# A two-layer stream encoder on one core: the guard of a hand-made instruction order counts engine time anew, the split of squares takes other tiles as room, and the start takes six small steps

## The chip, the cores and the metric

The kernel runs on one core of one Trainium2 chip. The metric is the device time of one execution in microseconds (us), as the median of several runs; lower is better.

## What is computed

The reference is an encoder of two layers on a sequence of 256 tokens of width 2048, all in float32. Cut to what matters:

```python
for l in range(2):
    h = rmsnorm(x, norm_mix[l])
    x = x + hybrid_mixer(h, ...)            # h @ w_in; three recurrences; concat([hg, ret, ssm]) @ w_out
    h = rmsnorm(x, norm_xattn[l]); m = rmsnorm(mem, norm_mem[l])
    x = x + memory_cross_attention(h, m)    # q = h @ wq; k, v = m @ wkv; softmax; @ wo
    x = x + conv_glu_ffn(rmsnorm(x, norm_ffn[l]))   # @ w_up, conv of 3 taps, silu(gate) * up, @ w_down
return rmsnorm(x, norm_final)
```

The mixer has three recurrences side by side: hg (a gated one), ret (a decaying one with rotary positions) and ssm. The output of each goes through a norm over groups before w_out.

## The kernel before, in words

**Work and stages.** Everything is kept transposed: channels on the 128 partitions, the 256 tokens in the free dimension. The weights, 479 MB in all, are streamed once from HBM through SyncE's DMA queue in groups of about 0.5 MB into five buffers `raw`. A float32 product is made of rounded pieces: ScalarE (ACT) rounds a piece of weights to `wh`, VectorE (DVE) subtracts to get the rest `wl`, and TensorE (PE) does, for each 128x128 block, one matmul of `wh` with 512 columns (the high and the low part of the activations beside each other) and one of `wl` with 256 columns. One such pair is called a pair below, one block of 128 channels of the input a k-tile.

**The order of the work.** The program is written out by hand, engine by engine; no scheduler moves anything, and every engine runs its own list in order. The main loop (from L1429) goes over some 890 steps, mostly of eight blocks: it issues the rounding of the weights of the step three ahead (`split_w_hi`, L1302) and the subtraction of the step two ahead (`split_w_lo`, L1310), which also loads a later group, then the step's matmuls, and then lets everything else move on by one piece. Because `wh` has five buffers and `wl` four, `wh` for step j+3 can't be written before PE has finished step j-2. "Everything else" are Python generators: the evacuation of a finished product, a norm, a recurrence, the attention. `advance` (L341) calls each of them once per step, and each issues instructions up to its next `yield`.

**The guard.** `advance(False)` after a step skips a generator when the books say that ACT or DVE is more than `BACKLOG` = 10 us behind (L344); only evacuations of products are never skipped. The books are kept by `Metered` (L248), which adds for each instruction (columns + fixed) / rate, and by `step_done` (L351), which takes off the time of the step's matmuls, so many us for each block, and adds what is over to `late`. Where a matmul needs an input that no generator has issued yet, `need` (L357) calls `advance()` with the guard off until it is there, ahead of that matmul in all the lists; `pj` (L379) does the same when all five PSUM tiles for products are held.

**What the steps of the argument touch.** `gen_gstd` (L637) makes the norm over groups: it splits squares into a high and a low part, sums them over the partitions with two matmuls, and goes on into `newton` (L402: Ln and Exp on ACT, then three operations on DVE); `gen_out` (L614) then multiplies and splits the result into the inputs `mo` of w_out. `z_evac` (L819) holds the PSUM tiles of the products z4 to z7 until all of hg's outputs are issued (the flag `hgdone`). `gen_mem` (L1062) makes the normalized memory `mh` for k and v, two k-tiles from each fetched piece of `memT`; a piece goes into one of two buffers `ya`, and the fetch of the next but one is issued when both k-tiles are done. `gen_first` (L1396) makes the squares of x for the first norm, whose result R every product of the first layer's w_in is multiplied with. The tiles `pr` and `w` have two buffers each; `gen_out` uses `pr`, `newton` and the rotary part of `gen_ret` (L1001) use `w`. At the start the first `SINGLE` steps carry one k-tile instead of two; x is loaded in pieces by the same queue as the weights.

Of the kernel before, what the change touches and what calls it, by code (L numbers as in the profile page):

```python
# [5 lines left out]
F32R = mybir.dt.float32r  # L6
# [5 lines left out]
P = 128  # L12
T = 256
# [44 lines left out]
K16 = [list(range(8)), list(range(8, 16))]  # L58


SINGLE = 4


def layer_plan(l):
# [183 lines left out]
class Metered:  # L248


    def __init__(self, engine, rate, fixed, fast=()):
        self.engine, self.rate, self.fixed, self.fast, self.us = engine, rate, fixed, fast, 0.0

    def __getattr__(self, name):
        f = getattr(self.engine, name)
        if name == "preload_act_table_set":
            def g(*a):
                self.us += 1.28
                return f(*a)
            return g  # L260

        def g(out, *a, **k):
            n = 1
            for d in out.shape[1:]:
                n *= d
            self.us += (n / (2 if name in self.fast else 1) + self.fixed) / self.rate
            return f(out, *a, **k)  # L267
        return g


def build(tc, ws, xT, memT, par, con, masks, rot, dec, outT):
    nc = tc.nc
    act, dve, pe, gp = Metered(nc.scalar, 1200.0, 190), Metered(nc.vector, 960.0, 64, ("tensor_scalar",)), nc.tensor, nc.gpsimd

    pc = tc.alloc_tile_pool(name="const", bufs=1)
    pw = tc.alloc_tile_pool(name="weights", bufs=1)
# [46 lines left out]
    def tmp(tag, shape, dt=F32, bufs=2):  # L323
        return pt.tile(shape, dt, name=nm(tag), tag=tag, bufs=bufs)
# [9 lines left out]
    def start(g, first=False):  # L334

        if first:
            gens.insert(sum(f for _, f in gens), (g, True))
        else:
            gens.append((g, False))
# [28 lines left out]
    def take(n):  # L368
        while free["ms"] < n:
            yield  # L370
        free["ms"] -= n
# [26 lines left out]
    def tt(out, a, b, op):  # L398
        dve.tensor_tensor(out, a, b, op)


    def newton(v, out):  # L402

        fn(out, v, AF.Ln)
        fn(out, out, AF.Exp, scale=-0.5)
        yield
        t = tmp("w", [P, 2, T])
        t = t[:, 0, :] if len(v.shape) == 2 else t
        dve.scalar_tensor_tensor(t, out, -0.5, out, ALU.mult, ALU.mult)
        tt(t, t, v, ALU.mult)  # L410
        dve.scalar_tensor_tensor(out, t, 1.5, out, ALU.add, ALU.mult)
# [66 lines left out]
    lock = {}  # L478
# [67 lines left out]
    def layer(l):  # L546
# [89 lines left out]

        def gen_gstd(sq, n, v, out):  # L637

            while lock.get("pr", 0):
                yield  # L640
            lock["pr"] = 2
            hl = [tmp("pr", [P, 2, T], F32R, bufs=2) for _ in range(2)]
            split_ones(sq, *hl)
            yield
            yield from take(1)
            ps = bank()
            sum_ones(ps.rearrange("p (i t) -> p i t", i=2), *hl)
            lock["pr"] = 0
            yield
            dve.tensor_scalar(v, ps.rearrange("p (i t) -> p i t", i=2), 1.0 / n, EPS, ALU.mult, ALU.add)  # L650
            give()
            yield
            yield from newton(v, out)
# [347 lines left out]
        def gen_ret(p):  # L1001
# [10 lines left out]
            for name in ("rq", "rk"):  # L1012
                yield from wait((A, name, b0), (A, name, b1))
                if "R" not in ret:
                    ret["R"] = 1
                    tt(ret["cs"], ret["cs"], R.unsqueeze(1).to_broadcast([P, 2, T]), ALU.mult)
                U = pg[name][:, b0:b0 + 2, :]

                W = tmp("w", [P, 2, T])
                for o in (0, 64):  # L1020
                    act.copy(W[o:o + 64], U[64 - o:128 - o])
                tt(U, U, ret["cs"][:, 0:1, :].to_broadcast([P, 2, T]), ALU.mult)
                tt(W, W, ret["cs"][:, 1:2, :].to_broadcast([P, 2, T]), ALU.mult)
                tt(U, U, W, ALU.add)
                yield
# [4 lines left out]
            for i in range(2):  # L1030
                a = b0 + i
# [278 lines left out]
    def split_w_lo(j):  # L1310
        if j < len(steps):
            st = steps[j]
            n = st["n"]
            st["wl"] = pw.tile([P, WMAX], F32R, name=nm("wl"), tag="wl", bufs=4)
            tt(st["wl"][:, :n], st["raw"], st["wh"][:, :n].bitcast(F32), ALU.subtract)
            if j + 1 == len(steps) or steps[j + 1]["g"] != st["g"]:
                load(st["g"] + 5)
            if j < 4:
                nc.sync.dma_start(X[2 + j // 2][:, j % 2 * 2:j % 2 * 2 + 2, :], xT[:, 8 + 2 * j:10 + 2 * j, :])

    begins = {}
    done = []
# [43 lines left out]
    with tc.manual_schedule():  # L1366
# [5 lines left out]
        def loadx(q, a, b):  # L1372
            q.dma_start(X[a // 4][:, a % 4:(b - 1) % 4 + 1, :], xT[:, a:b, :])
# [3 lines left out]
        act.preload_act_table_set("silu_and_others")  # L1377
        table[0] = "silu_and_others"
        load(1)
        for a, b, g in ((2, 3, 2), (3, 4, 3), (4, 6, 4), (6, 8, None)):  # L1380
            loadx(nc.sync, a, b)
            if g:
                load(g)

        warm = bank()
        for _ in range(NWARM):
# [33 lines left out]
            flags.add("lb")  # L1420
            yield

        start(gen_first())
        for j in range(2):
            first_h(j)
            split_w_hi(j)
# [2 lines left out]
        for j, st in enumerate(steps):  # L1429
# [8 lines left out]
                start(ev(ps), True)  # L1438
            done.clear()
            matmuls(st)  # L1440
            if j == 5:
                fn(ONES, one, AF.Copy)
                nc.sync.dma_start(CON, con)
# [7 lines left out]
            if j == 15:  # L1451
                start(gen_lb())
            advance(False)
            step_done(st["n"] / P * 0.325)
        for ev, ps in done:
            start(ev(ps))
        start(gen_rstd((("Z",), "acc"), ACC, R, None, ("RZ",)))
# [36 lines left out]
```

## Time and profile before

| what | value |
|---|---|
| median of 3 runs | 2571.05 us (2569.22 to 2572.76) |
| the profiled execution | 2572.93 us, its span 2571.1 us |
| mean granted clock of TensorE | 0.996 of full speed |
| busy, share of the span | PE 99%, DVE 75%, ACT 57% |

The span runs from the first to the last instruction; the execution's time has some 2 us around it. A row of the timeline gives the start, the duration, the engine and what is written from what; in brackets stands the idle time of the engine before it and what ended it.

### The profile page before, as it was taken

What the parts mean: (1) busy time and instruction counts of PE and PEld (TensorE: products, weight loads), DVE (VectorE), ACT (ScalarE), POOL (GpSimd) and SP (SyncE); (2) the same over time, 40 slices, a digit from 0 to 9 for tenths busy, and PEclk for the clock granted to TensorE, in tenths of its full rate; (3) what the DMA queues carried; (4) which work ended last, traced back from release to release, by engine and by line L of the source; (5) the groups of instructions that cost most, each with busy time, mean ns of one, the idle gap of its engine ahead of it and who ended that gap; (6) DMA issues with size and microseconds to landing.
All of it is one profiled execution on the core that took longest, in us unless ns stands there. A gap on an engine that the chain in (4) does not pass through costs nothing.

```text
span 2571.1 us, 40478 instructions
## 1 busy us (share of the span) xinstructions
PE 2547.1 (99%) x15584; PEld 2259.8 (88%) x15584; DVE 1927.2 (75%) x3034; ACT 1469.6 (57%) x2154; POOL 5.0 (0%) x12
## 2 busy tenths in 40 slices
PE   9999999999999999999999999999999999999998
PEld 8888978898888888888898888889988888888887
DVE  6898788768776567776678888876787765677765
ACT  6766566566555345555466665655655543555543
POOL 0000000000000000000000000000000000000000
PEclk9999999999999999999999999999999999999999
DMA  7556555656665666666665576565666666666664
GB/s 265 163 172 203 192 171 189 192 170 189 190 191 181 194 194 189 191 189 188 191 184 161 154 235 186 184 217 169 181 189 190 192 182 193 193 189 192 190 184 130
DMA packets 141105, 482.03 MB, mean 187 GB/s; under 512 B 15280, under 2 KB 21360, under 8 KB 140912
## 3 DMA queue, kind: packets, MB, share of 16 engines
q1 hardware_dynamic: 140624, 479.17, 60.2%
q8 instruction: 123, 2.02, 0.3%
q14 instruction: 70, 0.57, 0.1%
q10 hardware_dynamic: 288, 0.27, 0.0%
HBM read 477.25 MB, written 2.13 MB: 186 GB/s over the span
## 4 chain that ended last, share of the span: by engine, by line
PE 97%; DVE 2%; DMA 0%; ACT 0%; issue 0%; DVEq 0%; SPq 0%; ACTq 0%
PE pj L1339 57%; PE pj L1340 29%; PE pj L1360 2%; PE pj L1361 2%; PE pj L1362 2%; PE pj L1342 1%; PE pj L1343 1%; PE pj L1344 1%; PE ms L694 1%; DVE wl L267 0%; PE ms L777 0%; PE ms L943 0%; DVE w L267 0%; PE ms L1131 0%; PE ms L1165 0%; DMA raw<-ws 0%
## 5 line engine op out<-in xcount | busy, mean ns | idle before, releaser
L1339 PE MATMUL pj<-H,wh 128*128 128x512 f32 x4480 | 1563.3, 393 | 1.6 <-DVE H L267 1.6
L267 DVE TENSOR_TENSOR wl<-raw,wh 128x1024 fp32r<-128x1024 f32 (+2 forms) x894 | 1076.1, 1206 | 420.8 <-PE pj L1340 221.6
L267 ACT ACTIVATE wh<-raw 128x1024 fp32r<-128x1024 f32 (+2 forms) x894 | 934.6, 1048 | 659.0 <-PE pj L1339 349.7
L1340 PE MATMUL pj<-H,wl 128*128 128x256 f32 x4480 | 1254.4, 280 | 3.4 <-DVE wl L267 3.4
L1339 PEld LDWEIGHTS pj<-H,wh 128*128 128x128 f32 x4480 | 842.0, 188 | 188.3 <-DVE H L267 1.4
L1340 PEld LDWEIGHTS pj<-H,wl 128*128 128x128 f32 x4480 | 842.1, 188 | 5.2 <-DVE wl L267 4.7
L1339 PE MATMUL pj<-g,wh 128*128 128x512 f32 x1386 | 480.7, 392 | 0.0
L1340 PE MATMUL pj<-g,wl 128*128 128x256 f32 x1386 | 387.7, 280 | 0.0
L1339 PEld LDWEIGHTS pj<-g,wh 128*128 128x128 f32 x1386 | 260.2, 188 | 57.5
L1340 PEld LDWEIGHTS pj<-g,wl 128*128 128x128 f32 x1386 | 260.2, 188 | 0.0
L267 ACT COPY e<-pj 128x256 f32<-128x256 f32 x288 | 106.4, 370 | 240.9 <-PE pj L1340 235.1
L1339 PE MATMUL pj<-mo,wh 128*128 128x512 f32 x512 | 180.6, 396 | 5.4 <-DVE mo L267 5.4
L267 DVE SCALAR_TENSOR_TENSOR ya<-UPAD,PAR,ya 128x256 f32<-128x256 f32 x352 | 146.4, 478 | 0.0
L1340 PE MATMUL pj<-mo,wl 128*128 128x256 f32 x512 | 144.4, 282 | 0.0
L267 DVE TENSOR_TENSOR X<-X,pj 128x256 f32<-128x256 f32 x167 | 69.9, 420 | 82.9 <-PE pj L1340 73.3
L1339 PEld LDWEIGHTS pj<-mo,wh 128*128 128x128 f32 x512 | 97.5, 190 | 27.4 <-DVE mo L267 5.7
L1340 PEld LDWEIGHTS pj<-mo,wl 128*128 128x128 f32 x512 | 97.5, 190 | 0.1
L267 ACT ACTIVATE ya<-UPAD,PAR 128x256 f32<-128x256 f32 x176 | 94.9, 588 | 1.2 <-DVE g L267 1.2
L267 DVE TENSOR_TENSOR UPAD<-pj,e 128x256 f32<-128x256 f32 x208 | 86.3, 417 | 0.3
L267 DVE TENSOR_TENSOR UPAD<-UPAD,R 128x512 f32<-128x512 f32 (+1 forms) x120 | 74.3, 621 | 4.0
L1360 PE MATMUL pj<-wh,H 128*128 128x264 f32 (+1 forms) x256 | 73.3, 286 | 0.0
L1362 PE MATMUL pj<-wh,H 128*128 128x264 f32 (+1 forms) x256 | 72.7, 284 | 0.0
(278 smaller groups left out, 1969.7 us busy)
## 6 DMA issues: line engine op xcount, KB each, us to landing
raw<-ws SPq DMA_DIRECT2D x778, 512.0 KB, 4.0
raw<-ws SPq DMA_DIRECT2D x96, 448.0 KB, 3.4
raw<-ws SPq DMA_DIRECT2D x16, 528.0 KB, 4.0
DE<-CD SPq DMA_DIRECT2D x8, 512.0 KB, 4.8
ya<-memT SPq DMA_DIRECT2D x16, 256.0 KB, 4.3
DS<-CD SPq DMA_DIRECT2D x8, 256.0 KB, 5.8
X<-xT SPq DMA_DIRECT2D x6, 256.0 KB, 7.2
outT<-y SPq DMA_DIRECT2D x3, 512.0 KB, 2.8
```

Of the source, the lines that this page charges most:

```text
L267: return f(out, *a, **k)
L694: pe.matmul(b[r:r + 64, q * 64:(q + 1) * 64], ks[:, o:o + 64], qs[:, o:o + 64], start=True, stop=True)
L1339: pe.matmul(ps, wh[:, a], s, start=first, stop=False)
L1340: pe.matmul(ps[:, :T], wl[:, a], s[:, :T], start=False, stop=last)
L1342: pe.matmul(ps[:, :T], wh[:, a], s[:, :T], start=first, stop=False)
L1343: pe.matmul(ps[:, :T], wh[:, a], s[:, T:], start=False, stop=False)
L1344: pe.matmul(ps[:, :T], wl[:, a], s[:, :T], start=False, stop=last)
L1360: pe.matmul(ps, xh, wh[:, a], start=f, stop=False)
L1361: pe.matmul(ps, xh, wl[:, a], start=False, stop=False)
L1362: pe.matmul(ps, xl, wh[:, a], start=False, stop=e)
```

## The change

It has four parts. `gen_gstd` no longer takes both `pr` tiles but two `w` tiles for the split squares, and a new lock makes `newton` and the rotary part wait while it has them. `Metered` counts a fixed 240 instead of 190 cycles for an ACT instruction and 150 instead of 64 for one on DVE, no longer counts `tensor_scalar` at half, and a step pays off 0.347 instead of 0.325 us for each block. The first wave has six steps with one k-tile instead of four, with x loaded in smaller pieces between the weights. The squares of x start at step 6 instead of before step 0.

```diff
--- before.py
+++ after.py
@@ -58,7 +58,7 @@
 K16 = [list(range(8)), list(range(8, 16))]
 
 
-SINGLE = 4
+SINGLE = 6
 
 
 def layer_plan(l):
@@ -248,8 +248,8 @@
 class Metered:
 
 
-    def __init__(self, engine, rate, fixed, fast=()):
-        self.engine, self.rate, self.fixed, self.fast, self.us = engine, rate, fixed, fast, 0.0
+    def __init__(self, engine, rate, fixed):
+        self.engine, self.rate, self.fixed, self.us = engine, rate, fixed, 0.0
 
     def __getattr__(self, name):
         f = getattr(self.engine, name)
@@ -263,14 +263,14 @@
             n = 1
             for d in out.shape[1:]:
                 n *= d
-            self.us += (n / (2 if name in self.fast else 1) + self.fixed) / self.rate
+            self.us += (n + self.fixed) / self.rate
             return f(out, *a, **k)
         return g
 
 
 def build(tc, ws, xT, memT, par, con, masks, rot, dec, outT):
     nc = tc.nc
-    act, dve, pe, gp = Metered(nc.scalar, 1200.0, 190), Metered(nc.vector, 960.0, 64, ("tensor_scalar",)), nc.tensor, nc.gpsimd
+    act, dve, pe, gp = Metered(nc.scalar, 1200.0, 240), Metered(nc.vector, 960.0, 150), nc.tensor, nc.gpsimd
 
     pc = tc.alloc_tile_pool(name="const", bufs=1)
     pw = tc.alloc_tile_pool(name="weights", bufs=1)
@@ -404,6 +404,8 @@
         fn(out, v, AF.Ln)
         fn(out, out, AF.Exp, scale=-0.5)
         yield
+        while lock.get("w"):
+            yield
         t = tmp("w", [P, 2, T])
         t = t[:, 0, :] if len(v.shape) == 2 else t
         dve.scalar_tensor_tensor(t, out, -0.5, out, ALU.mult, ALU.mult)
@@ -636,16 +638,16 @@
 
         def gen_gstd(sq, n, v, out):
 
-            while lock.get("pr", 0):
-                yield
-            lock["pr"] = 2
-            hl = [tmp("pr", [P, 2, T], F32R, bufs=2) for _ in range(2)]
+            yield from take(1)
+            while lock.get("w"):
+                yield
+            lock["w"] = 1
+            hl = [tmp("w", [P, 2, T], F32R) for _ in range(2)]
             split_ones(sq, *hl)
             yield
-            yield from take(1)
             ps = bank()
             sum_ones(ps.rearrange("p (i t) -> p i t", i=2), *hl)
-            lock["pr"] = 0
+            lock["w"] = 0
             yield
             dve.tensor_scalar(v, ps.rearrange("p (i t) -> p i t", i=2), 1.0 / n, EPS, ALU.mult, ALU.add)
             give()
@@ -1014,6 +1016,8 @@
                 if "R" not in ret:
                     ret["R"] = 1
                     tt(ret["cs"], ret["cs"], R.unsqueeze(1).to_broadcast([P, 2, T]), ALU.mult)
+                while lock.get("w"):
+                    yield
                 U = pg[name][:, b0:b0 + 2, :]
 
                 W = tmp("w", [P, 2, T])
@@ -1315,8 +1319,9 @@
             tt(st["wl"][:, :n], st["raw"], st["wh"][:, :n].bitcast(F32), ALU.subtract)
             if j + 1 == len(steps) or steps[j + 1]["g"] != st["g"]:
                 load(st["g"] + 5)
-            if j < 4:
-                nc.sync.dma_start(X[2 + j // 2][:, j % 2 * 2:j % 2 * 2 + 2, :], xT[:, 8 + 2 * j:10 + 2 * j, :])
+            if j < 6:
+                a = (5, 6, 8, 10, 12, 14, 16)[j:j + 2]
+                nc.sync.dma_start(X[a[0] // 4][:, a[0] % 4:a[0] % 4 + a[1] - a[0], :], xT[:, a[0]:a[1], :])
 
     begins = {}
     done = []
@@ -1377,10 +1382,9 @@
         act.preload_act_table_set("silu_and_others")
         table[0] = "silu_and_others"
         load(1)
-        for a, b, g in ((2, 3, 2), (3, 4, 3), (4, 6, 4), (6, 8, None)):
-            loadx(nc.sync, a, b)
-            if g:
-                load(g)
+        for a in (2, 3, 4):
+            loadx(nc.sync, a, a + 1)
+            load(a)
 
         warm = bank()
         for _ in range(NWARM):
@@ -1420,7 +1424,6 @@
             flags.add("lb")
             yield
 
-        start(gen_first())
         for j in range(2):
             first_h(j)
             split_w_hi(j)
@@ -1438,6 +1441,8 @@
                 start(ev(ps), True)
             done.clear()
             matmuls(st)
+            if j == SINGLE:
+                start(gen_first())
             if j == 5:
                 fn(ONES, one, AF.Copy)
                 nc.sync.dma_start(CON, con)
@@ -1451,7 +1456,7 @@
             if j == 15:
                 start(gen_lb())
             advance(False)
-            step_done(st["n"] / P * 0.325)
+            step_done(st["n"] / P * 0.347)
         for ev, ps in done:
             start(ev(ps))
         start(gen_rstd((("Z",), "acc"), ACC, R, None, ("RZ",)))
```

How the lists move is shown at three places; the number behind a tile's name tells one use of it from another, and the number is not the same in the two programs. Steps are counted from 0.

First, DVE's list in the first layer where hg's outputs are normalized (`VV`, `w`, `RR`: Newton; `pr`, `mo`: the outputs; `xbc`, `UPAD`: the convolution of ssm; `z1`: the products z4 to z7). Before, from step 66 on:

```order
L267 TENSOR_TENSOR wl_70_2345<-raw_70_2183,wh_70_2307 128x1024
L267 SCALAR_TENSOR_TENSOR xbc3_1_2204<-UPAD1_110,PAR_78,xbc3_1_2204 128x256 x3
L267 TENSOR_TENSOR UPAD1_110<-pj_32_2252,e_28_2331 128x256
L267 TENSOR_TENSOR UPAD1_110<-UPAD1_110,R_102 128x256
L267 SCALAR_TENSOR_TENSOR w_3_2371<-RR_1_2107 128x512
L267 TENSOR_TENSOR w_3_2371<-w_3_2371,VV_1_2106 128x512
L267 SCALAR_TENSOR_TENSOR RR_1_2107<-w_3_2371,RR_1_2107 128x512
L267 SCALAR_TENSOR_TENSOR pr_6_2376<-OG_1_2105,HGW_108,RR_1_2107 128x256 x2
L267 TENSOR_TENSOR wl_71_2381<-raw_71_2216,wh_71_2343 128x1024
L267 TENSOR_TENSOR mo_1_2337<-pr_5_2338,mo_1_2337 128x2x256
L267 TENSOR_TENSOR wl_72_2410<-raw_72_2250,wh_72_2379 128x1024
L267 SCALAR_TENSOR_TENSOR xbc3_1_2204<-UPAD1_110,PAR_78,xbc3_1_2204 128x256 x3
```

Now, all of it ahead of the first matmul of step 83 (the first of rv):

```order
L267 TENSOR_SCALAR VV_1_2678<-ms_17_2710 128x512
L267 SCALAR_TENSOR_TENSOR w_6_2716<-RR_1_2679 128x512
L267 TENSOR_TENSOR w_6_2716<-w_6_2716,VV_1_2678 128x512
L267 SCALAR_TENSOR_TENSOR RR_1_2679<-w_6_2716,RR_1_2679 128x512
L267 SCALAR_TENSOR_TENSOR pr_1_2721<-OG_1_2677,HGW_108,RR_1_2679 128x256 x2
L267 SCALAR_TENSOR_TENSOR w_7_2727<-RR_1_2679 128x512
L267 TENSOR_TENSOR w_7_2727<-w_7_2727,VV_1_2678 128x512
L267 SCALAR_TENSOR_TENSOR RR_1_2679<-w_7_2727,RR_1_2679 128x512
L267 SCALAR_TENSOR_TENSOR pr_2_2732<-OG_1_2677,HGW_108,RR_1_2679 128x256 x2
L267 TENSOR_TENSOR mo_1_2720<-pr_1_2721,mo_1_2720 128x2x256
L267 TENSOR_TENSOR mo_2_2731<-pr_2_2732,mo_2_2731 128x2x256
L267 TENSOR_TENSOR z1_1_2738<-pj_37_2458,e_33_2739 128x256
```

Before, one or two operations stood between the subtractions `wl` of two steps, spread over steps 60 to 69; now hg's two halves stand in one run without a `wl` between them, at step 83, and the evacuation of z4 stands behind them.

Second, DVE's list at the w_out wave of the first layer, whose steps read `mo` two at a time (`w`, `rk`, `zsq`: Newton; `rA`, `ya`, `DE`: pieces of ret and ssm). Before, at its last steps:

```order
L267 TENSOR_TENSOR mo_7_3958<-pr_17_3959,mo_7_3958 128x2x256
L267 TENSOR_TENSOR pr_19_4009<-rk_1_3292,pr_18_4008 128x512
L267 TENSOR_TENSOR wl_122_4014<-raw_122_3877,wh_122_3985 128x1024
L267 TENSOR_TENSOR wl_123_4039<-raw_123_3912,wh_123_4012 128x1024
L267 TENSOR_SCALAR rA0_1_2495<-ms_39_4034 128x512
L267 TENSOR_TENSOR wl_124_4062<-raw_124_3938,wh_124_4037 128x1024
L267 SCALAR_TENSOR_TENSOR w_11_4069<-rk_1_3292 128x512
L267 TENSOR_TENSOR w_11_4069<-w_11_4069,rA0_1_2495 128x512
L267 SCALAR_TENSOR_TENSOR rk_1_3292<-w_11_4069,rk_1_3292 128x512
L267 TENSOR_TENSOR rq_1_3165<-rq_1_3165,rg_1_3676 128x256 x2
L267 SCALAR_TENSOR_TENSOR pr_20_4076<-rq_1_3165,PAR_78,rk_1_3292 128x256 x2
L267 TENSOR_TENSOR mo_8_4075<-pr_20_4076,mo_8_4075 128x2x256
```

Now, ahead of its third step:

```order
L267 SCALAR_TENSOR_TENSOR w_17_3874<-rk_1_3222 128x512
L267 TENSOR_TENSOR w_17_3874<-w_17_3874,rA0_1_2753 128x512
L267 SCALAR_TENSOR_TENSOR rk_1_3222<-w_17_3874,rk_1_3222 128x512
L267 TENSOR_TENSOR rq_1_3108<-rq_1_3108,rg_1_3594 128x256 x2
L267 SCALAR_TENSOR_TENSOR pr_4_3890<-xbc0_1_1336,PAR_78,zsq_1_3521 128x256 x2
L267 TENSOR_TENSOR rA0_1_2753<-ms_34_3880,rA0_1_2753 128x256
L267 TENSOR_TENSOR ya_2_2754<-ms_34_3880,ya_2_2754 128x128
L267 TENSOR_TENSOR rA0_1_2753<-ms_35_3881,rA0_1_2753 128x256
L267 TENSOR_TENSOR ya_2_2754<-ms_35_3881,ya_2_2754 128x128
L267 TENSOR_TENSOR DE_1_3054<-DE_1_3054,DS_1_3055 128x1024
L267 TENSOR_TENSOR mo_3_3870<-pr_3_3871,mo_3_3870 128x2x256
L267 TENSOR_TENSOR wl_121_3923<-raw_121_3713,wh_121_3840 128x1024
```

Before, only `mo_8`, the last input, was made ahead of the matmul that needs it, at the last step; now `mo_3` and the work before it stand there at the third step, and the same happens again at the fifth (some 30 instructions of ACT and DVE for `mo_5`, with two pairs of sums on PE among them).

Third, DVE's list at the memory's norm in the first layer (`mh` from `ya`; `RM` sums the squares). Before, from step 130 on:

```order
L267 SCALAR_TENSOR_TENSOR mh_2_4337<-ya_4_4083,PAR_78,mh_2_4337 128x256
L267 TENSOR_TENSOR RM_103<-RM_103,sq_24_4339 128x256
L267 TENSOR_TENSOR wl_134_4372<-raw_134_4229,wh_134_4341 128x1024
L267 TENSOR_TENSOR wl_135_4400<-raw_135_4257,wh_135_4370 128x1024
L267 SCALAR_TENSOR_TENSOR H7_93<-X1_83,PAR_78,H7_93 128x256
L267 TENSOR_TENSOR ACC_104<-ACC_104,sq_25_4393 128x256
L267 TENSOR_TENSOR X2_84<-X2_84,pj_65_4347 128x256 x2
L267 SCALAR_TENSOR_TENSOR mh_2_4337<-ya_4_4083,PAR_78,mh_2_4337 128x256
L267 TENSOR_TENSOR RM_103<-RM_103,sq_26_4396 128x256
L267 TENSOR_TENSOR wl_136_4429<-raw_136_4285,wh_136_4398 128x1024
L267 TENSOR_TENSOR wl_137_4460<-raw_137_4314,wh_137_4427 128x1024
L267 SCALAR_TENSOR_TENSOR H8_94<-X2_84,PAR_78,H8_94 128x256
```

Now, between the matmuls of steps 155 and 156 (the product k):

```order
L267 SCALAR_TENSOR_TENSOR mh_2_4992<-ya_4_4068,PAR_78,mh_2_4992 128x256
L267 TENSOR_TENSOR RM_103<-RM_103,sq_34_4994 128x256
L267 SCALAR_TENSOR_TENSOR mh_2_4992<-ya_4_4068,PAR_78,mh_2_4992 128x256
L267 TENSOR_TENSOR RM_103<-RM_103,sq_35_5001 128x256
L267 SCALAR_TENSOR_TENSOR mh_3_5009<-ya_5_4990,PAR_78,mh_3_5009 128x256
L267 TENSOR_TENSOR RM_103<-RM_103,sq_36_5011 128x256
L267 SCALAR_TENSOR_TENSOR mh_3_5009<-ya_5_4990,PAR_78,mh_3_5009 128x256
L267 TENSOR_TENSOR RM_103<-RM_103,sq_37_5018 128x256
L267 SCALAR_TENSOR_TENSOR mh_4_5026<-ya_6_5007,PAR_78,mh_4_5026 128x256
L267 TENSOR_TENSOR RM_103<-RM_103,sq_38_5028 128x256
L267 SCALAR_TENSOR_TENSOR mh_4_5026<-ya_6_5007,PAR_78,mh_4_5026 128x256
L267 TENSOR_TENSOR RM_103<-RM_103,sq_39_5035 128x256
```

Before, a k-tile of memory was made in every second step, over steps 124 to 155; now none is made until step 154, and 16 in a row follow there, each just ahead of the two matmuls that read it. In the second layer nine of the 16 k-tiles stand so.

## Rows read from the trace of the kernel before

**Rows 1.** The page's busy times, share of the span and instructions of each engine.
```profile
PE 2547.1 (99%) x15584; PEld 2259.8 (88%) x15584; DVE 1927.2 (75%) x3034; ACT 1469.6 (57%) x2154; POOL 5.0 (0%) x12
```
**Rows 2.** PE's waits: us in total, times, longest.
```profile
PE pj L1339 <- DVE mo L267: 5.4, 1, 5.4
PE pj L1340 <- DVE wl L267: 3.4, 4, 1.1
PE pj L1339 <- DVE H L267: 1.6, 2, 1.1
```
**Rows 3.** Timeline of the start, 10 to 19 us.
```profile
10.50 1.06 ACT L267 ACTIVATE wh<-raw 128x1024 fp32r<-128x1024 f32 x1 [1.47 <-DMA raw<-ws]
...
12.84 0.51 PE L1339 MATMUL pj<-H,wh 128*128 128x512 f32 x1 [1.12 <-DVE H L267]
...
14.37 0.39 PE L1340 MATMUL pj<-H,wl 128*128 128x256 f32 x1 [1.03 <-DVE wl L267]
...
14.60 0.43 PE L1339 MATMUL pj<-H,wh 128*128 128x512 f32 x1
...
18.24 0.41 PE L1339 MATMUL pj<-H,wh 128*128 128x512 f32 x1
...
18.60 0.39 PE L1339 MATMUL pj<-H,wh 128*128 128x512 f32 x1
...
18.95 0.40 PE L1339 MATMUL pj<-H,wh 128*128 128x512 f32 x1
```
**Rows 4.** Timeline at the last step of the first layer's w_out wave, 374 to 392 us.
```profile
375.44 1.06 ACT L267 ACTIVATE wh<-raw 128x1024 fp32r<-128x1024 f32 x1 [1.71 <-PE pj L1339]
...
376.52 1.28 ACT L259 ACT_TABLE_LOAD   x1
...
377.82 0.63 ACT L267 ACTIVATE rk<-rA 128x512 f32<-128x512 f32 x1
...
378.50 0.28 PE L1340 MATMUL pj<-mo,wl 128*128 128x256 f32 x1
...
383.44 0.69 DVE L267 TENSOR_TENSOR mo<-pr,mo 128x512 fp32r<-128x512 f32 x1 [0.69 <-ACT mo L267]
...
384.19 0.80 PE L1339 MATMUL pj<-mo,wh 128*128 128x512 f32 x1 [5.41 <-DVE mo L267]
...
390.12 0.48 PE L1339 MATMUL pj<-mo,wh 128*128 128x512 f32 x1
```
**Rows 5.** Busy us (instructions) by stretch, then PE's clock, DMA share, GB/s.
```profile
120.00:160.00 40.00, 40.00 (x330) 34.89 (x327) 38.68 (x61) 25.56 (x36) 0.00 (x0) 1.00 0.49 158
...
378.00:386.00 8.00, 2.59 (x10) 2.01 (x9) 5.49 (x10) 2.66 (x4) 0.00 (x0) 0.84 0.44 132
386.00:400.00 14.00, 14.00 (x71) 12.19 (x70) 11.08 (x21) 8.36 (x16) 0.00 (x0) 0.85 0.48 134
```
**Rows 6.** Groups of instructions by shape: count, busy us, mean ns, idle before.
```profile
L267 DVE TENSOR_TENSOR wl<-raw,wh 128x1024 fp32r<-128x1024 f32 x778 | 948.5, 1222 | 325.7 <-PE pj L1340 179.7 <-issue 114.6 <-PE pj L1361 7.4
...
L267 ACT ACTIVATE mh<-ya,PAR 128x256 fp32r<-128x256 f32 x32 | 15.8, 494 | 0.0
L267 DVE SCALAR_TENSOR_TENSOR mh<-ya,PAR,mh 128x256 fp32r<-128x256 f32 x32 | 15.3, 479 | 0.0
...
L267 DVE TENSOR_SCALAR DE<-DE,CUM 128x128 f32<-128x128 f32 x32 | 9.0, 281 | 3.3 <-DMA DE<-CD 3.3
...
L267 ACT ACTIVATE zsq<-zsq 128x512 f32<-128x512 f32 x8 | 5.1, 633 | 0.1
...
L267 DVE TENSOR_TENSOR hf<-hf,R 128x256 f32<-128x256 f32 x8 | 3.1, 422 | 0.1
...
L267 DVE SCALAR_TENSOR_TENSOR RR<-w,RR 128x512 f32<-128x512 f32 x4 | 2.8, 692 | 0.1
```
**Rows 7.** The chain that ended last: start us, us, what.
```profile
188.09 2.68 PE ms L777 x24
```
**Rows 8.** Fetches of `memT`, by tile.
```profile
DMA to landing us min/median/max: 3.9/4.3/5.9
```

## The prediction

> **What bounds the kernel now.** I read the page's busy times first: PE is busy for 2547 of 2571 us [rows 1], so a change can win little and lose much, and what counts is whether PE has to wait more or less than now. Next come PE's waits [rows 2]. Almost all lie at two places: the start, where two waits of about 1.1 us follow each other because weights and x are late [rows 3], and one wait of 5.41 us at the last step of the first layer's w_out wave [rows 4]. Then the timeline at that place. PE's last matmul there begins at 378.50. What comes next needs the last tile `mo`, and its whole chain was issued at one spot by `need`: ACT rounds the next `wh` as soon as PE frees the buffer (375.44), loads a table, does Ln and Exp from 377.82, DVE follows with Newton and the product, and `mo` is there at 384.13 [rows 4]. So a chain that the program lists directly ahead of the matmul that needs it isn't hidden. Last, the stretches: the clock granted after this wait is 0.84 and 0.85 of full speed [rows 5], that is some 6.8 us at 1.2 GHz in place of 2.4 GHz; from 384.19 to 390.12 PE takes nine pairs in 5.93 us, where a pair takes 0.35 us at full clock (18.60 to 18.95 [rows 3]), so 2.8 us more are lost. The shorter waits of the start cost 1.5 in the same way (14.60 to 18.24: six pairs in 3.64 us [rows 3]). I price a long wait with 2.8 and a short one with 1.5 us of slow clock on top.
>
> **The change part by part.** PE's matmuls are the same in number and shape, so only waits can move.
>
> *The start.* Six small steps let PE work on one k-tile at a time until more has landed. The fifth step's weights are now 0.25 MB in place of 0.5 and come earlier than 10.50 [rows 3]; the squares no longer stand between on ACT. What is late next is the seventh step (the first with two k-tiles): its `wl` stands behind four operations on x on DVE, and I leave 0.9 us of waiting there. The two waits (2.15 us) and their slow clock (1.5) shrink to that: 2.9 us gained, between 0 and 3.7.
>
> *The guard.* A wide subtraction takes 1222 ns [rows 6]; the old books said 1133 (1024 + 64 over 960), the new ones 1223. A 256-wide one takes 422 ns; the old said 333, the new 423. So the prices become right, while a step pays off 7% more. But DVE is busy 38.7 of 40 us in the first layer's recurrences [rows 5], and by right prices it is then nearly always 10 us behind. Generators are skipped, and what they should have done is issued later in one piece by `need` or `pj`, with the guard off. Such a piece itself counts as a backlog that the books work off by little more than 1 us a step (2.78 less the subtraction, 1.22), although PE has stood still meanwhile; so the next generators are held back for some ten steps or more and the next piece follows. The lists show it at seven places, against two without much behind them before. Each costs its serial chain less the work that PE has within it; widths of 512 take 0.69 us on DVE and 0.63 on ACT, of 256 about 0.42 to 0.49 [rows 6].
>
> 1. *First product hg (step 29).* Because the squares start late, R comes late. From PE's end of step 27: one subtraction, then 13 operations of 256 columns, 1.2 + 13 x 0.42 = 6.7; PE has a step of 2.8 and a little to do. Wait 3.5, clock 1.5: **5.0**.
> 2. *Ahead of rv (step 83).* The PSUM tiles of z4 to z7 wait for all of hg. After 2.7 us of matmuls of PE [rows 7] the chain is square, split, sums, split, scale, Ln, Exp, Newton, two products, Newton, two products, round, and the copy and add of z4: with four wide ACT operations before the first Newton, about 16.3 us in all. PE has 6.8 of its own (the 2.7, the two pairs of sums, transposes, the first of rv). Wait 9.5, clock 2.8: **12.3**.
> 3. *The w_out wave of the first layer (steps 117 and 119).* At 117: DVE's 12 decay operations at 0.28 reach to 4.8; then two Newtons of 2.1, three pairs of 256-wide products, four short operations, one wide and one half-wide, until 15.0; PE has 3.5 of it: wait 11.5. At 119: two norms in series with their splits and sums, 14.8, less 1.2 of PE: 13.6. Clock twice 2.8. The 5.4 and 2.8 of now are saved, since the last `mo` comes in the same piece. 11.5 + 13.6 + 5.6 - 8.2 = **22.5**.
> 4. *Memory of the first layer (steps 155, 156).* All 16 k-tiles, with the Newton for q's R ahead of the second, which is there at 6.9. Only two pieces of `memT` are in the buffers, and each further fetch waits for the k-tiles of the piece two before. A turn is one landing (3.9 at least, 4.3 the median, most of them in layer 1: 4.1 [rows 8]), two roundings with a square between and a subtraction (0.49 + 0.42 + 0.49 + 0.48): 6.0. The odd pieces go 8.7, 14.7, 20.7, 26.7, and one fetch stands on SyncE behind a load of weights that waits for a `wl`: 1.5 more. 28.2 less PE's 16 pairs (5.6): wait 22.6, clock 2.8: **25.4**.
> 5. *Attention of the first layer (step 171).* The norm of memory, all four heads and their outputs are one chain, but PE has ten groups of matmuls in it. I bound it by 0 and by place 7 (9) and take 5.0, the middle; clock 1.5: **6.5**.
> 6. *The w_out wave of the second layer (steps 565 to 568).* At its end nearly the chain of now stands again, 6.37 us from Ln to PE's start (377.82 to 384.19 [rows 4]) plus the scaling, 0.7; at the second step before, 2.3. Wait 9.4, clock 2.8: **12.2**.
> 7. *Memory of the second layer (steps 601, 602).* Nine k-tiles are left; pieces at 3.0, then two turns of 4.3 + 1.5: 14.6, less 5.6: 9.0, clock 2.8: **11.8**.
>
> The Trainium skill (ScalarE: Activation LUTs, "What ACT_TABLE_LOAD costs") puts every switch of tables at 2.66 us, with a drain of 1.38 behind the load. Here the load starts at 376.52, right behind the rounding, and Ln starts 1.30 later [rows 4]; so I count 1.3. By the page, places 3 and 6, which have a switch in their chains, would be 1.4 longer each, and the sum 2.8 higher.
>
> *The split in `w` tiles.* It removes the wait for both `pr` tiles and adds one: two halves now wait for each other's sums, and Newton for the lock. In pieces issued at once this is in the chains above; elsewhere DVE has other work, and I count 0, between -1 and +3 (one Newton and a half).
>
> Sum: 5.0 + 12.3 + 22.5 + 25.4 + 6.5 + 12.2 + 11.8 - 2.9 = 92.8 us. The profiled execution took 2572.93, so 2665.7; the median of the runs lies 1.9 below that execution: **2664 us**, 3.6% slower.
>
> **The rivals.**
> *A, the guard does what it is for: faster.* If the pieces run beside PE's own work, because DVE, no longer overloaded, has its inputs ready early, only the 5.4 + 2.8 us of the wave and 2.9 of the start change: 2571 - 11 = 2560. It decides at place 2: if the chain from hg's matmuls to z4 fits into the 6.8 us PE has, A holds. Against it stands the wait of now, where a chain of half that length wasn't hidden [rows 4]. The Trainium skill (VectorE: DVE Perf Modes, "The TRN2 errata") gives an fp32 tensor_tensor (N + 151)/0.96 ns, which is the new price; by it the books are true, and holding back by true books should smooth the work. The trace agrees on the price (1222 ns). Chance 4%.
> *B, no difference.* Pieces and savings cancel within 0.2% (5 us, about what a measurement of this kernel can tell from no change): 2571. It asks for chains of a tenth of those above. Chance 2%.
> *C, only norms cost.* If a fetch of memory lands while the one before is worked on and isn't held by its buffer, places 4 and 7 fall to a few us: 2664 - 31 = 2633. For it: landings are short when PE stands. Against it: two buffers, each freed by its last subtraction. Chance 14%.
> *D, more waits than listed.* Places that the lists don't mark, where small matmuls of PE stand one step behind their inputs on an overfull DVE, and the slow clock lasting through the sparse stretches: a third more, 2664 + 31 = 2695. For it: every chain above is made of durations alone, without the time from one engine to the next. Chance 25%.
>
> **How the numbers follow.** My own sum holds 55%. The waits of the seven places are 84.1 us and their slow clock 19.8; a fourth less of the one and half of the other is 2664 - 21 - 10 = 2633, a third more and half as much again 2664 + 28 + 10 = 2702. C and D reach about as far, so the range is 2625 to 2705, with A, B and what lies outside on either side left out. Faster by more than 0.2%: 0.04 (A); within 0.2%: 0.02 (B); slower: 0.94.
>
> **What would show it.** PE's waits after should sum to 75 to 105 us in place of the 10.4 shown [rows 2], led by `mh` and `mo` of DVE and by PSUM tiles behind z; the clock should be about 0.99 or less in the mean; timelines should show waits of some 10 us ahead of rv and at the third and fifth step of the first wave, and in the first layer's k a saw-tooth of pairs behind landings of `memT` every 3 us. The start should show no wait above 1 us. It would be wrong if PE runs through the first rv without a wait, or if memory's 16 k-tiles take under 10 us.

## The result, and the profile after

The changed kernel takes **2661.6 us** (median of 4 runs, 2660.9 to 2663.2) against 2571.9 for the kernel before beside it: 1.035 times as long, 95% interval 1.0335 to 1.0366. The forecast was 2664, between 2625 and 2705. The profiled span is 2660.3 us, 89.2 longer than that of before.

The page of the changed kernel, its busy times and the granted clock in 40 slices:

```profile
span 2660.3 us, 40519 instructions
...
PE 2576.5 (97%) x15584; PEld 2275.0 (86%) x15584; DVE 1931.4 (73%) x3035; ACT 1476.6 (56%) x2157; POOL 4.9 (0%) x12
...
PEclk9999988989999999999999999999999999999999
```

PE has the same 15584 matmuls as before [rows 1], but is busy 29.4 us longer, and it stands still for 2660.3 - 2576.5 = 83.8 us in place of 24.0. The dents in the clock are in the first layer. What PE waits for, in total, times and the longest, of the changed kernel:

```profile
PE pj L1344 <- DVE mo L267: 20.0, 3, 8.9
PE pj L1344 <- DVE mh L267: 15.3, 11, 3.1
PE ms L779 <- DVE rA L267: 13.3, 1, 13.3
PE pj L1365 <- DVE z L267: 8.0, 1, 8.0
PE ms L421 <- ACT w L267: 5.0, 3, 3.6
PE ms L1159 <- ACT pr L267: 2.7, 2, 2.1
PE pj L1344 <- DVE hg L267: 2.1, 1, 2.1
```

These replace the short list of [rows 2]. To see what each place costs I set every matmul of a product beside the same one in the trace before (14,614 records in both) and read how far it is displaced: -3.0 us at record 384, behind the start; 9.6 at 1680, behind places 1 and 2; 38.0 at 2064, behind the first w_out wave; 57.3 at 2592 and 65.8 at 2928, behind memory and attention of the first layer; still 65.8 at 8208, so that the rest of the layer loses nothing; 81.3 at 9360 and 88.9 at 11160, behind places 6 and 7. The waits in the table are those of over 0.15 us, which the list of PE's waits has for each stretch.

| place | forecast: waits, with clock | waits after | displaced by |
|---|---|---|---|
| start | -2.9 in all | | -3.0 |
| 1 and 2: first hg, ahead of rv | 13.0, 17.3 | 12.0 | 12.6 |
| 3: first w_out wave | 25.1 less 5.4, 22.5 | 26.3 | 28.4 |
| 4: memory, first layer | 22.6, 25.4 | 11.4 | 19.3 |
| 5: attention, first layer | 5.0, 6.5 | 3.6 | 8.5 |
| 6: second w_out wave | 9.4, 12.2 | 11.2 | 15.5 |
| 7: memory, second layer | 9.0, 11.8 | 3.8 | 7.6 |
| sum | 92.8 | | 88.9 |

Record 1680 does not part places 2 and 3 cleanly. Of PE's small matmuls (`ms`), 374 stand ahead of it in the kernel before and 336 in the changed one; the other 38, which take some 4 us in the trace before, have moved behind it. Without that shift places 1 and 2 cost about 16.6 us and place 3 about 24.4. At 2064 the counts are equal again.

Place 2 in the chain of the changed kernel (start, us, what), from hg's last matmuls to the first of rv:

```profile
248.17 2.69 PE ms L779 x24
250.86 0.02 issue
250.88 0.61 ACT SQ L267
251.49 0.02 issue
251.51 0.69 DVE OG L267
252.20 0.61 DVE w L267
...
262.94 0.69 DVE mo L267
263.64 0.34 DVE z L267
263.98 0.04 issue
264.03 0.58 PE pj L1365
```

Nearly every link of the chain that the prediction wrote down stands there, each starting about 0.02 us after the one before has ended; PE's sums are not among them, and the product `OG` of DVE is. It takes 15.8 us from 248.17 to 263.98, forecast 16.3. The waits in it are 1.2 and 8.0 us, 9.2 against 9.5.

Place 3 in the timeline of the changed kernel:

```profile
374.43 0.42 SPq L913 DMA_DIRECT2D DS<-CD  x1
...
378.88 0.28 DVE L267 TENSOR_SCALAR DE<-DE,CUM 128x128 f32<-128x128 f32 x1 [2.47 <-DMA DE<-CD]
...
380.20 0.29 DVE L267 TENSOR_SCALAR DS<-DS,CUM 128x128 f32<-128x128 f32 x1 [0.84 <-DMA DS<-CD]
...
389.21 1.19 PE L779 MATMUL ms<-rA,rv 128*128 128x256 f32 x2 [13.29 <-DVE rA L267]
...
414.09 0.79 PE L1344 MATMUL pj<-mo,wh 128*128 128x512 f32 x1 [8.95 <-DVE mo L267]
```

The first of the two waits has a part that the prediction doesn't have: DVE itself waits 2.47 + 0.84 = 3.3 us for the decay factors, whose two fetches are issued only at 373.96 and 374.43, directly ahead of the piece; the second takes 5.74. In the kernel before, this layer's last such fetch is issued at 313.88, some 60 us before the wave.

Place 4 in the timeline of the changed kernel, where k's products take the normalized memory `mh` from DVE:

```profile
519.49 0.47 PE L1344 MATMUL pj<-mh,wh 128*128 128x512 f32 x1 [1.75 <-DVE mh L267]
...
523.15 0.79 PE L1344 MATMUL pj<-mh,wh 128*128 128x512 f32 x1 [3.07 <-DVE mh L267]
...
525.93 0.51 ACT L267 ACTIVATE mh<-ya,PAR 128x256 fp32r<-128x256 f32 x1 [2.05 <-DMA ya<-memT]
...
530.35 0.51 ACT L267 ACTIVATE mh<-ya,PAR 128x256 fp32r<-128x256 f32 x1 [0.36 <-DMA ya<-memT]
...
534.82 0.51 ACT L267 ACTIVATE mh<-ya,PAR 128x256 fp32r<-128x256 f32 x1 [2.96 <-DMA ya<-memT]
...
535.36 0.49 DVE L267 SCALAR_TENSOR_TENSOR mh<-ya,PAR,mh 128x256 fp32r<-128x256 f32 x1 [2.92 <-ACT mh L267]
...
535.90 0.79 PE L1344 MATMUL pj<-mh,wh 128*128 128x512 f32 x1 [2.73 <-DVE mh L267]
...
539.43 0.51 ACT L267 ACTIVATE mh<-ya,PAR 128x256 fp32r<-128x256 f32 x1 [1.68 <-DMA ya<-memT]
```

The saw-tooth of pairs behind landings is there, but one buffer's fetches are issued at 523.17, 527.76 and 532.18: a turn takes 4.6 and 4.4 us, not 6.0. The other buffer's turns take 6.6 and 5.5; the first of these has in it the fetch that stands on SyncE behind a load of weights (530.77), as the prediction had it. The view of the tile memT in this stretch has the reason for the short turns:

```profile
DMA to landing us min/median/max: 2.6/2.8/3.8
```

Against 4.3 in the median before [rows 8]. Last, the granted clock by stretches (the number behind POOL's is the clock, 1.00 full, 0.50 the lower level):

```profile
378.83:392.49 13.66, 3.28 (x10) 2.85 (x11) 12.60 (x31) 5.77 (x9) 0.00 (x0) 0.50 0.14 44
...
402.73:419.79 17.06, 7.22 (x19) 5.41 (x20) 12.55 (x24) 5.67 (x9) 0.00 (x0) 0.50 0.10 31
519.00:541.00 22.00, 11.82 (x30) 7.10 (x30) 15.09 (x38) 13.06 (x34) 0.00 (x0) 0.61 0.29 96
```

Behind the start, the changed kernel has nine stretches at 0.50 in which PE works, 88.7 us in all; the kernel before has two, 10.2 us. The first line is the sum over the nine, the second that over the two:

```profile
sum 88.74, PE 49.64 PEld 39.30 DVE 63.78 ACT 38.66 POOL 0.00; mean PE 5.52 PEld 4.37 DVE 7.09 ACT 4.30 POOL 0.00
```

```profile
sum 10.23, PE 9.52 PEld 8.17 DVE 8.27 ACT 5.09 POOL 0.00; mean PE 4.76 PEld 4.09 DVE 4.14 ACT 2.54 POOL 0.00
```

### The profile page after: what moved, and what is told of

It is laid out like the page before. It is cut to its first block, busy times and chain, and to the rows that moved or that the text cites. A ratio compares the mean times of both kernels' runs of the same rounds, so it can differ in the third digit from the quotient of the medians.

```text
span 2660.3 us, 40519 instructions
## 1 busy us (share of the span) xinstructions
PE 2576.5 (97%) x15584; PEld 2275.0 (86%) x15584; DVE 1931.4 (73%) x3035; ACT 1476.6 (56%) x2157; POOL 4.9 (0%) x12
## 4 chain that ended last, share of the span: by engine, by line
PE 92%; DVE 5%; ACT 1%; DMA 1%; issue 0%; DVEq 0%; SPq 0%; ACTq 0%
PE pj L1344 54%; PE pj L1345 28%; PE pj L1365 2%; PE pj L1366 2%; PE pj L1367 2%; DVE wl L267 1%; DMA ya<-memT 1%; DVE w L267 1%; PE pj L1348 1%; PE pj L1349 1%; PE pj L1347 1%; DVE xbc L267 1%; PE ms L779 0%; PE ms L696 0%; DVE pr L267 0%
```

## Experiments

The theory: the new books hold generators back at a threshold of 10 us, and the work comes later in one piece directly ahead of the matmul that needs it; the late squares add pieces of their own. The rivals: late squares set everything off; the `w` tiles with their lock lengthen the chains; DVE is truly overloaded, whatever the books say. Times are medians; the kernel before ran beside each, at 2570.8 to 2571.2.

### The four parts apart

**The books alone**, in the kernel before:

```diff
-            self.us += (n / (2 if name in self.fast else 1) + self.fixed) / self.rate
+            self.us += (n + self.fixed) / self.rate
...
-    act, dve, pe, gp = Metered(nc.scalar, 1200.0, 190), Metered(nc.vector, 960.0, 64, ("tensor_scalar",)), nc.tensor, nc.gpsimd
+    act, dve, pe, gp = Metered(nc.scalar, 1200.0, 240), Metered(nc.vector, 960.0, 150), nc.tensor, nc.gpsimd
...
-            step_done(st["n"] / P * 0.325)
+            step_done(st["n"] / P * 0.347)
```

> The kernel before with the new books alone (fixed 240 and 150, no half price, 0.347 a block); start, squares and pr tiles as before. My theory, that the loss comes from generators held back by the new books and issued in one piece ahead of the matmul that needs them: no piece at the first hg, a small one ahead of rv, the pieces of the first w_out wave, of the first layer's memory and attention, and of the second layer's w_out wave and (five k-tiles) memory stay. With what these places cost in the changed kernel (about 28, 19, 9, 15 and 5 us, and 1 ahead of rv) it comes to 2572 + 77 = 2649 us, between 2630 and 2665. The rival that the late squares make every later stage late: 2585 or less. The rival that the w tiles make the chains long enough to show: well under 2630.

Measured: 2626.4 us, 1.0217 times before (1.0201 to 1.0233). The books cost 56 us by themselves; the rival of the late squares (2585) falls. But the time lies 4 below the range of my theory. By the displaced matmuls everything up to the end of the first w_out wave costs only 8.9 here (from -1.7 at record 384 to 7.2 at 2064), where 29 was expected: no wait stands ahead of rv, and without late squares the wave has one long wait (8.3) beside two of 3.9 and 1.2, not two long ones.

**All but the books**: the changed kernel with the lines marked - above. 

> The changed kernel with the old books. My theory: the start gains 3, the wait of the old wave (8.2 with its slow clock) goes, the late squares leave one piece at the first hg (3), a shorter one at the third step of the first w_out wave (16 operations on DVE, some 12) and three late k-tiles of memory (5): 2572 - 11 + 20 = 2581 us, between 2570 and 2592. The rival that the late squares are the cause: 2630 or more, near the changed kernel's 2662. The rival of the w tiles: over 2600 too.

Measured: 2590.0, 1.0076 (1.0064 to 1.0089), inside the range and 9 above the number. PE's waits of this kernel:

```profile
PE pj L1344 <- DVE mo L267: 8.6, 1, 8.6
PE pj L1344 <- DVE mh L267: 3.5, 3, 1.9
PE pj L1345 <- DVE wl L267: 3.3, 6, 1.1
PE pj L1344 <- DVE hg L267: 2.1, 1, 2.1
```

The three places that were named (hg, mo, three k-tiles of memory) and beside them little but `wl`, as before [rows 2]. So the late squares hurt without the new books too.

**The w tiles alone**, in the kernel before:

```diff
+            yield from take(1)
-            while lock.get("pr", 0):
+            while lock.get("w"):
...
-            lock["pr"] = 2
-            hl = [tmp("pr", [P, 2, T], F32R, bufs=2) for _ in range(2)]
+            lock["w"] = 1
+            hl = [tmp("w", [P, 2, T], F32R) for _ in range(2)]
```

> The kernel before with the split squares in w tiles and the lock alone. My theory: the one wait of 5.4 us at the end of the first w_out wave and its 2.8 us of slow clock go, nothing else is moved: 2572 - 8 = 2564 us, between 2560 and 2570. The rival that the lock makes Newton and the rotary part wait and lengthens the chains: 2575 or more.

Measured: 2563.7, 0.9972 (0.9962 to 0.9982): 7.1 us faster than before, and the first version that beats both kernels. Its list of PE's waits begins

```profile
PE pj L1344 <- DVE wl L267: 3.7, 5, 1.1
PE ms L1391 <- POOL UPAD L1372: 1.3, 1, 1.3
PE ms L434 <- ACT sq L267: 0.6, 1, 0.6
```

with no `mo` in it: the wait of 5.41 us [rows 4] is gone, and with the old books the lock costs nothing that shows.

**The w tiles and the six small steps**, with the squares before step 0 and the old books:

```diff
-SINGLE = 4
+SINGLE = 6
...
-        for a, b, g in ((2, 3, 2), (3, 4, 3), (4, 6, 4), (6, 8, None)):
+        for a in (2, 3, 4):
```

> The kernel before with the w tiles and with the six small steps and x between them, but with the squares before step 0 as before and the old books. My theory: the gains of both add, 8 from the wave and 3 from the start: 2561 us, between 2556 and 2567; it beats both kernels. The rival that the start gains only because the squares are out of its way: 2564 as with the w tiles alone. The rival of the lock: 2572 or more.

Measured: 2564.5, 0.9976 (0.9967 to 0.9985). The gains don't add: the small steps give nothing on top of the w tiles (2563.7). Three us at the start were a matter of the one execution that was profiled: in the kernel with the w tiles alone, whose start is that of before, the wait for H is already absent.

```profile
12.12 0.51 PE L1343 MATMUL pj<-H,wh 128*128 128x512 f32 x1 [0.27 <-DVE H L267]
13.65 0.39 PE L1344 MATMUL pj<-H,wl 128*128 128x256 f32 x1 [1.03 <-DVE wl L267]
```

Above is that kernel's timeline; in the kernel before the first of the two was 1.12 long, and the clock dropped behind it [rows 3]. At record 48 the kernels with the old start (books alone, w tiles alone) stand 2.3 us ahead of that profile, as the changed one does; at record 384 they are 1.7 and 1.8 ahead, the changed one 3.0.

### Squares, books and threshold

**The changed kernel with the squares before step 0 again:**

```diff
+        start(gen_first())
         for j in range(2):
...
-            if j == SINGLE:
-                start(gen_first())
```

> The changed kernel with the squares of x before step 0 again (small steps, w tiles and new books stay). My theory of pieces: the ones at the first hg and ahead of rv go, the first w_out wave has one large piece in place of two, everything behind it stays; so what the late squares cost on top of the books is the places 1 and 2 (13) and part of the wave (10 to 20): 2662 - 13 - 15 = 2634 us, between 2618 and 2645. The rival that the lateness of R sets off the whole row of pieces: 2600 or less. The rival that late squares cost the same 25 with either books: 2637, inside my range; then their cost is no matter of the books.

Measured: 2631.7, 1.0236 (1.0221 to 1.0251). The late squares cost 29.9 with the new books and 2590.0 - 2564.5 = 25.5 with the old: mostly an addition of their own, as the last rival says, though not by the same waits. With the new books the displaced matmuls put 17 us at places 1 and 2 and 12 at the wave; with the old ones some 14 lie at the wave and 6 at memory. One row also bears on the fetch at place 3: in this kernel the decay factors are fetched long ahead, at about 339 us, and the wait for the same product is

```profile
PE ms L779 <- DVE rA L267: 7.5, 1, 7.5
```

in place of 13.3. The fetch doesn't explain all of that difference, since two shorter waits (1.7 and 0.8) stand ahead of this one.

The same kernel once more (its label speaks of a threshold, but that was not changed) says, in a single run, only how well a time repeats:

> The same kernel as the one with the squares before step 0, for a second look at its trace: the same time within 5 us.

Measured: 2632.1, 0.4 from the median above.

**The false backlog.** The changed kernel, where `need` and `pj` set the books to zero after a piece (n counts the calls of `advance` that it took):

```diff
+    def forget(n):
+        if n:
+            for k, e in (("dve", dve), ("act", act)):
+                late[k] = e.us = 0.0
...
+        forget(n)
```

> The changed kernel, but after each piece that is issued with the guard off the books of ACT and DVE are set to zero, since PE stood still meanwhile. My theory, that a piece's own time counts as a backlog that isn't there and holds back what makes the next piece: the first of the two pieces of the first w_out wave goes, and so do those of memory and attention (places 4, 5 and 7, some 19, 9 and 8 us in the changed kernel); the pieces at the first hg, ahead of rv, the second of the wave and those of the second layer's wave stay: 2662 - 36 - 10 = 2616 us, between 2603 and 2632. The rival, that DVE is truly overloaded there and the pieces come without any false books: 2650 or more.

Measured: 2615.2, 1.0172 (1.0157 to 1.0187). PE's waits:

```profile
PE pj L1351 <- DVE mo L267: 16.2, 3, 7.3
PE pj L1372 <- DVE z L267: 8.3, 1, 8.3
PE ms L786 <- DVE rA L267: 7.5, 1, 7.5
PE pj L1351 <- DVE hg L267: 2.1, 1, 2.1
```

No wait for `mh` is left in either layer and none for the attention's `pr`, though not one instruction became cheaper. The wave's first piece, which was expected to go altogether, is only smaller (7.5 in place of 13.3). Half of the loss (46 of 90 us) thus goes when the books are emptied behind each piece. Emptying also takes away what backlog there truly was; the two weren't told apart.

**Memory never skipped**, otherwise the changed kernel:

```diff
-            start(gen_mem())
+            start(gen_mem(), True)
```

> The changed kernel, but the generator of the normalized memory is never skipped by the guard. My theory: only the last k-tile of memory is left at steps 156 and 602, the waits of places 4 and 7 go (19 and 8 us in the changed kernel, their slow clock among it), the others stay: 2635 us, between 2625 and 2645. The rival that the work of memory, issued earlier, makes the w_out wave later by as much: 2655 or more.

Measured: 2633.4, 1.0241 (1.0224 to 1.0258). Matmuls are displaced against the changed kernel by -19.0 us behind place 4 and a further -7 behind place 7, and by less than 1.3 through the first wave: memory's work costs nothing when it comes in its own time. 

**Threshold 30**, with early squares and with late:

```diff
-BACKLOG = 10.0
+BACKLOG = 30.0
```

> The changed kernel with the squares before step 0 and with BACKLOG 30 in place of 10; prices and credit stay new. My theory, that the new prices do harm only through the threshold of 10 us: no piece but the last k-tile of memory in each layer is left, and the time is that of the kernel with the old books, small steps and w tiles: 2564.5 us, between 2560 and 2571. The rival, that the new prices or the credit bring waits by an order of their own whatever the threshold: 2580 or more.

> The changed kernel as it is, with BACKLOG 30 in place of 10. My theory: the pieces of the late squares stay (first hg, the third step of the first w_out wave, three k-tiles of memory in the first layer), those of the books go: as the changed kernel with the old books, 2590 us, between 2582 and 2598. The rival, that with late squares the backlog is real and a higher threshold only moves the waits: 2620 or more.

Measured: 2562.9, 0.9968 (0.9957 to 0.9980), and 2585.7, 1.0057 (1.0042 to 1.0073). The first keeps all new prices and is as fast as the w tiles alone. All six kernels below have the w tiles and the small steps:

| | old books, 10 | new books, 10 | new books, 30 |
|---|---|---|---|
| squares before step 0 | 2564.5 | 2631.7 | **2562.9** |
| squares at step 6 | 2590.0 | 2661.6 | 2585.7 |

The new books with their old threshold cost 67 to 72 us, the late squares 23 to 30, and the two nearly add. With the 7 that the w tiles give, and nothing from the small steps, that is -7 + 67 + 30 = 90, the whole difference; along this one path through the runs it closes by itself. The parts don't add in every order: the books alone cost 56 in the kernel before, and with them the w tiles and the small steps together make it 5.3 us slower (2631.7 against 2626.4), where with the old books they make it 6.3 faster. The displaced matmuls put 3.1 us of that at each of the two w_out waves; whether the lock or something else does it wasn't run. Nor were the parts of the books (fixed prices, half price, credit) run apart, and no run leaves the guard out, so that what it is good for at a threshold of 30 isn't known. The best kernel is the w tiles with squares before step 0, with old books or with new ones at a threshold of 30: some 8 us faster than before, 2562.9 or 2563.7, which these runs can't tell apart.

## Why the prediction was right

*The mechanism*: right. Seven places were named, and the displaced matmuls show losses at these and at no other. That pieces are made by the books, and that a piece's own time makes the next one, was forecast; the runs with the threshold at 30 and with the books set to zero show both. But only place 1 (5.0) was put down to the late squares, and the runs put 23 to 30 us to them. Place 2 needs them: its wait for `z` is absent with early squares, with the old books and with the threshold at 30. Of place 3, some 12 of its 28 us go with early squares.

*The sum*: 92.8 against 88.9 us, by errors that cancel. Waits at the seven places came to 68.5 us in place of 84.1, 15.6 fewer. PE's busy time grew by 29.4, where 15.5 of slow clock was forecast (19.8 less the 2.8 and 1.5 of before), 13.9 more. That the sum lies within 4 us is luck to that extent.

- Places 4 and 7, memory, were mis-sized: 25.4 and 11.8 against 19.3 and 7.6. The landing of a fetch was taken as 4.1 and 4.3 from [rows 8]; 2.8 and 3.1 were measured in the median, the first in a stretch where the DMA share is 0.29 and the queue carries little else, which is what rival C had in its favour. And I put the slow clock on top of the waits there; PE's pairs at half clock took up time in which it would have waited anyway.
- Place 3, the w_out wave, was too small: 22.5 against 28.4, or 24.4 without PE's small matmuls that moved there. The DMA that was moved along with the piece is missing in it, 3.3 us of DVE's waiting in a chain that was written with DVE's operations alone.
- Place 6 was too small by 3.3: I took the wave's last chain and one more wait; the waits were 3.82 and 7.19 against 9.4, the rest is slow clock.
- Place 5, taken as the middle between two bounds, was 6.5 against 8.5.
- Place 1 had a wait of 3.5, where 2.1 was measured; place 2 was right in nearly all its links, its length (15.8 against 16.3) and its wait.
- The start's 2.9 was seen in the profile (-3.0) and yet isn't the small steps' doing: it was read from one execution in which H came late. Two kernels with the old start show nearly the same. (Its own sum, 2.15 + 1.5 - 0.9, is 2.75.) The 1.9 by which the median lies below the profiled execution was taken off as well; it is probably the same late start counted twice, which no second profile of the kernel before can show.
- Not every wait of before lies at the two places that were named: two for `wl`, 1.1 us each, stand at 218.05 and 1474.18. They are gone in the changed kernel, a gain of some 2 us that the sum doesn't have.

Of the signs, the waits in the whole list come to 71.3 us, a little under the 75 to 105 that were named, and memory's turns are shorter than they were; the clock (0.982), the start, the places and their order are as forecast.

*The rivals.* A asked whether the chain to z4 fits into PE's work: 8.0 us of waiting at that place say no. The Trainium skill (VectorE: DVE Perf Modes, "The TRN2 errata") has (N + 151)/0.96 ns for an fp32 tensor_tensor. The trace agrees (1222 ns for 1024 columns, [rows 6]). The new books have 1223 for this instruction and are nearer to what was measured than the old with 1133. They still lose 67 us at a threshold of 10, and nothing at 30, so a true price didn't decide. The Trainium skill (ScalarE: Activation LUTs, "What ACT_TABLE_LOAD costs") has 2.66 us for every switch, a drain of 1.38 behind the load among it. The trace doesn't agree here: at place 3 the load starts at 376.73 and takes 1.28, and the next ACT instruction starts at 378.02. The term of 1.3 stands. D, that a third more would be lost, didn't come about: the displaced matmuls show no eighth place.

Most of PE's 29.4 us more is clock. Behind the start PE worked 49.6 us at the lower level, against 9.5 before; a pair takes some 0.7 us there and 0.35 at the higher one, so half of each is lost, some 20 us more (an estimate). At the start five pairs at 0.64 us in place of 0.35 add 1.5. What stays open: what the other 8 are, and why the same start has a late H in one execution and not in another wasn't looked into.

## What to carry to other kernels

A guard that holds work back by a model of engine time needs its threshold set together with its prices: truer prices with the old threshold made everything look late, and the delayed work came back as serial chains ahead of PE. Time that a forced piece takes while the main engine stands should be taken out of such books: here half of the loss came back when they were emptied behind each piece. And a gain read from waits of a single profiled execution, above all at the start where DMA sets the pace, should be looked up in a second one.

## What the runs showed of the hardware

The landing of a 256 KB piece of `memT` took 2.8 us in the median of six while PE stood between its pairs, against 4.3 [rows 8] with the stream of weights running. How long the slow clock lasts doesn't follow the length of the wait: after 13.29 us of waiting (until 389.21) the clock is back at full at 392.49, 3.3 us later; after 8.95 (until 414.09) only at 419.79, 5.7 later. And at the very start it may come up late without any long wait before it: in the changed kernel PE's pairs are 0.64 us apart until 9.86 and then 0.35, while in the kernel before they are 0.35 apart by 7.64.

```profile
7.72 0.41 PE L1345 MATMUL pj<-H,wl 128*128 128x256 f32 x1
...
8.36 0.41 PE L1345 MATMUL pj<-H,wl 128*128 128x256 f32 x1
...
10.25 0.28 PE L1345 MATMUL pj<-H,wl 128*128 128x256 f32 x1
...
10.61 0.28 PE L1345 MATMUL pj<-H,wl 128*128 128x256 f32 x1
```

These rows are of the changed kernel's timeline at the start, 0.64 us from pair to pair and then 0.36; that execution alone says little of what the small steps gain.
